# Seven matrix products for eight in more blocks of a hybrid GLA/gMLP layer, with PSUM sums copied from one bank into others

## The chip, the cores and the metric

The kernel runs on one core of one Trainium2 chip. The metric is device time in microseconds (us). Three runs of the kernel before gave 1591.32 us in the median, 1591.16 to 1591.44.

## The reference

One encoder layer on 256 tokens of width 2048, all in fp32. The parts that cost time are products of a 256-row activation with a wide weight matrix:

```python
proj = h @ w_in[i] + b_in[i]                      # 2048 x 14400
q, k, v, og, fg, u, z, ga, gb = jnp.split(proj, pts, axis=-1)
o = gla_chunk_causal(q, k, v, log_a)              # log_a from fg
y_a = rms_norm(o, gla_norm_g[i]).reshape(bsz, s, d) * jax.nn.silu(og)
y_b = gmlp_spatial_gate(gelu(u), gelu(z), gmlp_ln_g[i], gmlp_ln_b[i], w_s[i], b_s[i])
m = jax.nn.sigmoid(ga) * y_a + jax.nn.sigmoid(gb) * y_b
h = layer_norm(ALPHA * h + m @ w_o[i], ln1_g[i], ln1_b[i])      # 2048 x 2048
gt, up = jnp.split(h @ w_gu[i], 2, axis=-1)                     # 2048 x 11264
ffn = (jax.nn.silu(gt) * up) @ w_down[i]                        # 5632 x 2048
ple = jax.nn.sigmoid(h @ w_pg[i] + b_pg[i]) * (p[i] @ w_pu[i])  # 2048 x 2048
h = layer_norm(ALPHA * h + ffn + ple, ln2_g[i], ln2_b[i])
```

## The kernel before, in words

**Products.** Activations are held transposed, in k-tiles of 128 features by 256 tokens, so that a token tile t (0 or 1) of a k-tile is the 128x128 weight of a matmul and 512 columns of a weight matrix stream through. Each fp32 operand is cut into a high part and a low part of the type that TensorE takes (fp32r); a product is three matmuls, high by high, low by high, high by low (`mm3`, lines 275 to 278, and `mul`, 390 to 398).

**Weights.** A weight chunk is two k-tiles by 512 columns (128x1024 in SBUF, 512 KB from HBM, queue SP). Two chunks share one "raw" buffer. `cut` (197 to 204) makes the high part on ScalarE (line 202) and the low part on VectorE (line 203) into a buffer `w`. Raw, cut and long-lived buffers come from one pool of 21 slots.

**Steps.** All work with weights is a list of steps, each with a split (what the cut does) and a use (its matmuls). `pump` (253 to 270) goes through the steps in order. Before the use of step c it emits splits of later steps as long as at most `limit["hl"]` cut buffers are held, and loads as long as at most `limit["raw"]` raw buffers are; after the use it emits one or two jobs. A job is mostly an evacuation: VectorE and ScalarE take a finished PSUM sum, add a bias, apply a function, and so on. `before(c, fn)` puts other work ahead of step c. The queues of SP and GpSimd run as written; ScalarE's up to step 230, which is the end of ga; the rest is put in order by the toolchain, by priority.

**Blocks.** The order is v, fg, q, k, og, z, u, gb, ga, wo, pu, pg (each 2048 columns in four blocks of 512, but for fg, q, k, pu), then four parts of gate/up and down. `token_block` (280 to 333) keeps two PSUM sums, one per token tile, over 8 chunks of 12 matmuls. `pair_block` (366 to 540) takes 512 gate columns and 512 up columns together: four sums C11, C21, C12, C22 (token tile, column block) over 8 pairs of k-tiles. For two of the pairs (`s_gu = 2`, line 1221) it makes seven products in place of eight: it subtracts and adds the four 128x512 weight quarters on VectorE (lines 430, 460, 461), uses sums of the activations that `sums` (335 to 364) made once, and keeps a fifth sum V. What is common to several sums is copied from PSUM to SBUF by ScalarE (lines 451, 452, 512), joined on VectorE (453, 514), and added at each evacuation (1154, 1168). There are 11 such blocks in parts of 3, 3, 3 and 2, with four down blocks (12 or 8 k-tiles) behind each part. PSUM has five banks for these sums (`acc`) and three for the rest (`aux`).

**Around them.** `bcast` (104 to 107) loads 512 elements of a bias or gain to all partitions (three buffers). `residual` (624 to 631) multiplies and adds ln1's gain and bias on GpSimd, called from pg's evacuations (1140). At the start `keep_busy` (643 to 647) fills the wait for x with transposes of the identity.

Of the kernel before, what the change touches and what calls it, by code (L numbers as in the profile page):

```python
# [40 lines left out]
def block_kernel(ctx: ExitStack, tc: tile.TileContext, x, p, ln0_g, ln0_b, w_in, b_in, w_f2, b_f2,  # L41
# [322 lines left out]
    def pair_block(srcs, nk, xT, evacs, name, s, sT):  # L366
# [17 lines left out]
        def bank(key):  # L384
            first = key not in B
            if first:
                B[key] = acc(f"{name}_{key}")
            return B[key], first

        def mul(key, x, w):  # L390
            ps, first = bank(key)
            for j, ((xh, xl), (wh, wl)) in enumerate(zip(x, w)):
                nc.tensor.matmul(ps, lhsT=xh, rhs=wh, start=first and j == 0, stop=False,  # L393
                                 skip_group_check=True)
                nc.tensor.matmul(ps, lhsT=xl, rhs=wh, start=False, stop=False,  # L395
                                 skip_group_check=True)
                nc.tensor.matmul(ps, lhsT=xh, rhs=wl, start=False, stop=True,  # L397
                                 skip_group_check=True)
# [16 lines left out]

        def done(key, t, c):
            left[key] -= 1
            if left[key] == 0:
                add_out(key, B[key], t, c)


        def a1(i, raw):
# [18 lines left out]

        def a2(i, raw, need):
            def split():
                return cut(raw.tile.rearrange("p (q c) -> p q c", c=CB)[:, 0:4:2, :], f"{name}_b{i}")

            def use(w):
                mul("C21", [SX(2, i)], [W(w, 1)])
                mul("C12", [SX(0, i)], [W(w, 0)])
                if i == s - 1:
                    p1, p7 = t2(f"{name}_p1"), t2(f"{name}_p7")  # L450
                    nc.scalar.activation(p1, B["V"], AF.Copy)
                    nc.scalar.activation(p7, B["C21"], AF.Copy)
                    nc.vector.tensor_tensor(out=p7, in0=p7, in1=B["C12"], op=ALU.add)
                    st["p1"], st["h"] = p1, p7
            add_step(split, use, need)

        def tsum(i, raw):
            q = lambda j: raw.tile[:, j * CB:(j + 1) * CB]

            nc.vector.tensor_tensor(out=q(0), in0=q(0), in1=q(3), op=ALU.add)  # L460
            nc.vector.tensor_tensor(out=q(1), in0=q(1), in1=q(0), op=ALU.subtract)


        def std(i, order, sum_of=None):
            raw = Raw()
            n0 = add_half(raw, 0, srcs[0][:, 2 * i:2 * i + 2, :], 2, CB)
            n1 = add_half(raw, 1, srcs[1][:, 2 * i:2 * i + 2, :], 2, CB)
            keys = {(0, 0): "C11", (1, 0): "C21", (0, 1): "C12", (1, 1): "C22"}
            ws = {}

            def mk(c):
                def split():
                    w = cut(raw.tile[:, c * 1024:(c + 1) * 1024], f"{name}_c{i}_{c}")
                    if c == 1 and sum_of is not None:
                        tsum(*sum_of)
                    return w

                def use(w):
                    ws[c] = w
# [800 lines left out]
```

## Time and profile before

| | before |
|---|---|
| runs | 1591.32 us median of 3 (1591.16 to 1591.44) |
| profiled execution | 1591.31 us, its span 1589.5 us |
| mean granted TensorE clock | 0.996 |
| TensorE matmul busy | 1567.8 us, 7442 matmuls |
| VectorE, ScalarE, GpSimd busy | 1062.1, 747.1, 86.5 us |
| HBM read | 312.06 MB, 198 GB/s over the span |

The span is the time between the first and the last instruction that the profiler recorded; 1.8 us of the execution lie outside it. Matmuls overlap in the records (each shows 0.39 us), so the distance of their starts is what one costs, not its duration. VectorE's and ScalarE's instructions overlap by about 0.1 us when one follows another at once.

### The profile page before, as it was taken

Reading aid. Unit: us, or ns where it says so; the run is one execution under the profiler, and the core shown is the slowest. Engines: PE = TensorE matmul, PEld = TensorE weight load, DVE = VectorE, ACT = ScalarE, POOL = GpSimd, SP = SyncE. Lnnn points to the kernel's source line nnn. Section 1 sums busy time; section 2 is a strip of 40 time slices with the busy share of each in tenths; the row PEclk is TensorE's granted clock in tenths of the full one; section 3 lists DMA queues with packets and bytes.
Section 4 is the critical chain, followed back from the end, with each engine's and each line's share of the span. In section 5 each row is a group of like instructions: output and inputs, shape, how many; then the busy total and the mean of one; then the engine's idle time right before and its main releaser. Section 6 shows DMA issues by size and latency. Waiting matters only on the chain.

```text
span 1589.5 us, 19295 instructions
## 1 busy us (share of the span) xinstructions
PE 1567.8 (99%) x7442; PEld 1315.6 (83%) x7442; DVE 1062.1 (67%) x1219; ACT 747.1 (47%) x889; POOL 86.5 (5%) x69
## 2 busy tenths in 40 slices
PE   8999999999999999999999999999999999999996
PEld 7889988888888888888888888888888888888885
DVE  7658456467755556674899776577765777657775
ACT  5435446345543344462744554455544545435440
POOL 1021100001000000000142000000000000000002
PEclk9999999999999999999999999999999999999998
DMA  8664647566656665674577557555565645656551
GB/s 299 200 199 157 215 140 259 192 217 215 200 201 202 222 207 167 223 259 137 187 243 240 180 185 237 179 201 178 184 212 192 227 165 184 211 186 227 172 184 53
DMA packets 164598, 315.43 MB, mean 198 GB/s; under 512 B 10237, under 2 KB 13210, under 8 KB 164250
## 3 DMA queue, kind: packets, MB, share of 16 engines
q1 hardware_dynamic: 164442, 314.19, 58.9%
q8 instruction: 58, 0.95, 0.2%
q14 instruction: 34, 0.28, 0.1%
q10 hardware_dynamic: 64, 0.02, 0.0%
HBM read 312.06 MB, written 2.10 MB: 198 GB/s over the span
## 4 chain that ended last, share of the span: by engine, by line
PE 49%; issue 46%; DVE 3%; POOL 1%; DMA 1%; ACT 0%; SPq 0%; DVEq 0%; POOLq 0%; ACTq 0%
PE og L276 2%; PE v L277 2%; PE og L278 2%; PE v L278 2%; PE ga L278 2%; PE og L277 2%; PE wo L276 2%; PE z L278 2%; PE ga L277 2%; PE u L278 2%; PE wo L277 2%; PE z L277 2%; PE u L277 2%; PE gb L278 2%; PE gb L277 2%
## 5 line engine op out<-in xcount | busy, mean ns | idle before, releaser
L203 DVE TENSOR_TENSOR w_s<-raw,w_s 128x1024 fp32r<-128x1024 f32 x382 | 463.4, 1243 | 167.8 <-ACT w_s L202 167.4
L202 ACT ACTIVATE w_s<-raw 128x1024 fp32r<-128x1024 f32 x382 | 390.5, 1053 | 221.0 <-PE dn L278 72.4
L393 PE MATMUL gu_C<-gu_c_s,h1Th 128*128 128x512 f32 x528 | 205.4, 389 | 0.0
L395 PE MATMUL gu_C<-gu_c_s,h1Tl 128*128 128x512 f32 x528 | 205.4, 389 | 0.0
L397 PE MATMUL gu_C<-gu_c_s,h1Th 128*128 128x512 f32 x528 | 205.4, 389 | 0.0
L203 DVE TENSOR_TENSOR gu_c_s<-raw,gu_c_s 128x1024 fp32r<-128x1024 f32 x132 | 159.2, 1223 | 60.9 <-ACT gu_c_s L202 60.0
L202 ACT ACTIVATE gu_c_s<-raw 128x1024 fp32r<-128x1024 f32 x132 | 137.9, 1059 | 96.5 <-PE gu_C L397 49.3
L276 PE MATMUL dn<-w_s,act 128*128 128x512 f32 (+1 forms) x352 | 136.9, 389 | 0.0
L278 PE MATMUL dn<-w_s,act 128*128 128x512 f32 (+1 forms) x352 | 136.2, 387 | 0.0
L277 PE MATMUL dn<-w_s,act 128*128 128x512 f32 (+1 forms) x352 | 136.1, 387 | 0.0
L397 PEld LDWEIGHTS gu_C<-gu_c_s,h1Th 128*128 128x128 f32 x528 | 99.1, 188 | 20.6
L393 PEld LDWEIGHTS gu_C<-gu_c_s,h1Th 128*128 128x128 f32 x528 | 99.1, 188 | 20.6
L395 PEld LDWEIGHTS gu_C<-gu_c_s,h1Tl 128*128 128x128 f32 x528 | 99.1, 188 | 20.6
L278 PEld LDWEIGHTS dn<-w_s,act 128*128 128x128 f32 x352 | 66.1, 188 | 13.5
L276 PEld LDWEIGHTS dn<-w_s,act 128*128 128x128 f32 x352 | 66.1, 188 | 13.5 <-ACT act L575 0.3
L277 PEld LDWEIGHTS dn<-w_s,act 128*128 128x128 f32 x352 | 66.1, 188 | 13.3
L552 POOL TENSOR_TENSOR ln_r<-ln_v,mhalf 128x1 f32<-128x1 f32 x6 | 4.2, 693 | 1078.5 <-DVE ln_v L547 1078.5
L277 PE MATMUL v<-w_s,h0Tl 128*128 128x512 f32 x128 | 50.0, 391 | 0.9 <-POOL h0Tl L576 0.9
L276 PE MATMUL v<-w_s,h0Th 128*128 128x512 f32 x128 | 50.4, 394 | 0.0
L276 PE MATMUL ga<-w_s,h0Th 128*128 128x512 f32 x128 | 50.4, 394 | 0.0
L276 PE MATMUL og<-w_s,h0Th 128*128 128x512 f32 x128 | 50.2, 392 | 0.0
L276 PE MATMUL wo<-w_s,mTh 128*128 128x512 f32 x128 | 50.1, 391 | 0.0
(296 smaller groups left out, 3152.9 us busy)
## 6 DMA issues: line engine op xcount, KB each, us to landing
raw<-in_w_in_dram SPq DMA_DIRECT2D x226, 512.0 KB, 4.5
raw<-in_w_gu_dram SPq DMA_DIRECT2D x176, 512.0 KB, 4.4
raw<-in_w_down_dram SPq DMA_DIRECT2D x88, 512.0 KB, 4.9
raw<-in_w_o_dram SPq DMA_DIRECT2D x32, 512.0 KB, 5.1
raw<-in_w_pg_dram SPq DMA_DIRECT2D x32, 512.0 KB, 5.0
xs<-in_x_dram SPq DMA_DIRECT2D x4, 512.0 KB, 5.0
raw<-in_w_pu_dram SPq DMA_DIRECT2D x4, 512.0 KB, 4.6
out_dram<-xs SPq DMA_DIRECT2D x8, 256.0 KB, 2.1
```

Source lines behind the costliest of these rows:

```text
L202: nc.scalar.activation(hi, src, AF.Copy)
L203: nc.vector.tensor_tensor(out=lo, in0=src, in1=hi.bitcast(F32), op=ALU.subtract)
L276: nc.tensor.matmul(ps, lhsT=xh, rhs=wh, start=start, stop=False, **kw)
L277: nc.tensor.matmul(ps, lhsT=xl, rhs=wh, start=False, stop=False, **kw)
L278: nc.tensor.matmul(ps, lhsT=xh, rhs=wl, start=False, stop=stop, **kw)
L393: nc.tensor.matmul(ps, lhsT=xh, rhs=wh, start=first and j == 0, stop=False, skip_group_check=True)
L395: nc.tensor.matmul(ps, lhsT=xl, rhs=wh, start=False, stop=False, skip_group_check=True)
L397: nc.tensor.matmul(ps, lhsT=xh, rhs=wl, start=False, stop=True, skip_group_check=True)
L552: nc.gpsimd.tensor_tensor(out=r[:, :n], in0=v[:, :n], in1=mhalf[:, :n], op=ALU.pow)
```

## The change

`pair_block` is rewritten and used in more places. A pair of k-tiles with seven products is now five steps (`sa` to `se`). The product that all four sums share is made once in C12's bank; ScalarE copies C12's bank into the bank of C11 (`seed`), on which TensorE then accumulates, and later, with two further products in it, into the bank of C22; two partial sums go to SBUF (`keep`: `p7` from C21, `v` from C12) and are added at the evacuations of C22 and C21. C11 and C12 have nothing added. The fifth sum V is gone. The other pairs (`std`) are ordinary chunks, and the last chunk of a block is held back (`pending`) until the next block has emitted its `sa` steps (`flush`).

Seven products serve two pairs of k-tiles in og's second two blocks, in u and gb, in ga's first two, in pg's second two blocks, and three pairs in gate/up (before: two). z goes through `pair_block` with none (`S_Z = 0`). Two `sums` are made: of h0's k-tiles for the first, of h1's for pg and gate/up. `rowvec` loads 1024 elements at a time, at a set step ahead of the first use. Evacuations and the copies get a priority 150 instructions earlier. `residual` for ln1 is called at steps 5, 8, 11 and 14 of pg. z's norm takes two instructions in place of three. At the start, 20 fp32 matmuls of the identity go to the five banks in place of 14 transposes. ScalarE runs as written up to two steps before the end of og's first two blocks.

The core of the diff (what `pair_block` loses is printed above; lines that start with a blank stand in both):

```diff
+S_IN, S_Z, S_GA, S_PG, S_FF = 2, 0, 2, 2, 3
+SOON = 150
...
-    def bcast(src, c0, name, n=CB):
+    rows_t = {}
+
+    def rowvec(key, src, c0, b):
+
+        k = key, b // 2
+        if k not in rows_t:
+            rows_t[k] = tmp.tile([P, 2 * CB], F32, tag="bc", name=f"{key}{b // 2}", bufs=3)
+            o = c0 + b // 2 * 2 * CB
+            nc.sync.dma_start(rows_t[k], src[o:o + 2 * CB].partition_broadcast(P))
+        return rows_t[k][:, b % 2 * CB:(b % 2 + 1) * CB]
...
+    pending = []
+    def flush():
+        while pending:
+            pending.pop()()
-        while n > 0 and jobs:
-            jobs.popleft()()
-            n -= 1
+        with tc.high_priority(offset=SOON):
+            while n > 0 and jobs:
+                jobs.popleft()()
+                n -= 1
...
+        def seed(key):
+            B[key] = acc(f"{name}_{key}")
+            with tc.high_priority(offset=SOON):
+                nc.scalar.activation(B[key], B["C12"], AF.Copy)
+        def keep(key, nm):
+            st[nm] = t2(f"{name}_{nm}")
+            with tc.high_priority(offset=SOON):
+                nc.scalar.activation(st[nm], B[key], AF.Copy)
...
+        def done(key):
             left[key] -= 1
             if left[key] == 0:
+                t, c = int(key[1]) - 1, int(key[2]) - 1
+                jobs.append(lambda: evacs[c](t, B[key], st.get({"C21": "v", "C22": "p7"}.get(key))))
+        def q(i, j, n=1):
+            return raws[i].tile[:, j * CB:(j + n) * CB]
+        def sa(i):
+            add_half(raws[i], 0, srcs[0][:, 2 * i:2 * i + 2, :], 2, CB)
+            need_of[i] = add_half(raws[i], 1, srcs[1][:, 2 * i:2 * i + 2, :], 2, CB)
             def split():
+                w = cut(q(i, 0), f"{name}_a{i}", CB)
+                r = raws[i].tile.rearrange("p (q c) -> p q c", c=CB)
+                nc.vector.tensor_tensor(out=r[:, 0:4:2, :], in0=r[:, 0:4:3, :],
+                                        in1=r[:, 2, :].unsqueeze(1).broadcast_to([P, 2, CB]),
                                         op=ALU.subtract)
                 return w
             def use(w):
+                mul("C12", [X(i, 0, 0)], [W(w)])
+                if i == s - 1:
+                    seed("C11")
+            add_step(split, use, need_of[i])
+        def sb(i):
+            def p2(j):
+                mul("C11", [X(j, 1, 0)], [W(wb[j], 0)])
+                done("C11")
+            def use(w):
+                wb[i] = w
+                mul("C21", [SX(2, i)], [W(w, 1)])
+                if i:
+                    p2(i - 1)
+                if i == s - 1:
+                    keep("C21", "p7")
+                    p2(i)
+            n = add_step(lambda: cut(q(i, 1, 2), f"{name}_b{i}"), use, need_of[i], (),
+                         None if i == s - 1 else True)
+            if i:
+                steps[n]["free_hl"] += 1
+        def sc(i):
             def split():
+                nc.vector.tensor_tensor(out=q(i, 2), in0=q(i, 0), in1=q(i, 3), op=ALU.add)
+                w = cut(q(i, 2), f"{name}_c{i}", CB)
+                nc.vector.tensor_tensor(out=q(i, 1), in0=q(i, 1), in1=q(i, 2), op=ALU.subtract)
+                return w
             def use(w):
+                mul("C12", [SX(1, i)], [W(w)])
+                if i == s - 1:
+                    keep("C12", "v")
+            add_step(split, use, need_of[i])
+        def sd(i):
+            def use(w):
                 mul("C12", [SX(0, i)], [W(w, 0)])
                 if i == s - 1:
+                    seed("C22")
                 mul("C21", [X(i, 1, 1)], [W(w, 1)])
+                done("C21")
+            add_step(lambda: cut(q(i, 0, 2), f"{name}_d{i}"), use, need_of[i])
+        def se(i):
+            def use(w):
+                mul("C12", [SX(3, i)], [W(w)])
+                done("C12")
+            add_step(lambda: cut(q(i, 3), f"{name}_e{i}", CB), use, need_of[i], (raws[i],))
+        def std(i, c):
+            def consume(hi, lo):
+                w = [(hi[:, o * CB:(o + 1) * CB], lo[:, o * CB:(o + 1) * CB]) for o in range(2)]
+                for t in range(NT):
+                    mul(f"C{t + 1}{c + 1}", [X(i, 0, t), X(i, 1, t)], w)
+                    done(f"C{t + 1}{c + 1}")
+            add_chunk(srcs[c][:, 2 * i:2 * i + 2, :], 2, CB, consume)
+        c0 = [(lambda i=i: std(i, 0)) for i in range(s, npair)]
+        c1 = [(lambda i=i: std(i, 1)) for i in range(s, npair)]
         if s:
+            todo = [lambda i=i: sa(i) for i in range(s)] + [flush]
+            todo += [lambda i=i: sb(i) for i in range(s)]
+            todo.append(c0.pop(0))
+            todo += [lambda i=i: sc(i) for i in range(s)]
+            todo.append(c0.pop(0))
+            todo += [lambda i=i: sd(i) for i in range(s)]
+            for i in range(s):
+                if c0:
+                    todo.append(c0.pop(0))
+                todo.append(lambda i=i: se(i))
+                if len(c1) > 2 or not c0:
+                    todo.append(c1.pop(0))
+            todo += c0 + c1
+        else:
+            todo = [flush] + [f for x in zip(c0, c1) for f in x]
+        for f in todo[:-1]:
+            f()
+        pending.append(todo[-1])
...
+    def soon(n, fn):
+        before(len(steps) + n, fn)
+    def pairs(w, c0, xT, evac, name, s, sT, bs=(0, 2), vecs=()):
+        for b in bs:
+            for key, src, o in vecs:
+                soon(8, lambda key=key, src=src, o=o, b=b: rowvec(key, src, o, b))
+            pair_block((wcols(w, c0 + b * CB), wcols(w, c0 + (b + 1) * CB)), KT, xT,
+                       (evac(b), evac(b + 1)), f"{name}{b}", s, sT)
...
-        keep_busy(14, "busy0")
+        banks = [acc(f"init{i}") for i in range(5)]
+        for j in range(4):
+            for i in range(5):
+                nc.tensor.matmul(banks[i][:, j * P:(j + 1) * P], lhsT=ident, rhs=ident,
+                                 start=j == 0, stop=j == 3, skip_group_check=True)
...
+        nc.vector.tensor_tensor(out=a, in0=ps, in1=rowvec(f"b_{key}", src, c0, b), op=ALU.add)
+    soon(4, lambda: rowvec("b_og", b_in, C_OG, 0))
+    for b in range(2):
+    n_act = len(steps) - 2
+    before(len(steps) - 3, lambda: G.update(s0=sums(h0T, S_IN, "s0")))
+    before(len(steps), lambda: limit.update(raw=4, hl=5))
+    pairs(w_in, C_OG, h0T, og_evac, "og", S_IN, s0, (2,), [("b_og", b_in, C_OG)])
+                                           in1=rowvec("gmg", gm_g, 0, b), op0=ALU.subtract,
+                                           in1=rowvec("gmb", gm_b, 0, b), op0=ALU.mult, op1=ALU.add)
...
+            later(7, parts)
+            later(11, mix)
+    pairs(w_in, C_Z, h0T, z_evac, "z", S_Z, s0, (0, 2), [("b_z", b_in, C_Z), ("gmg", gm_g, 0), ("gmb", gm_b, 0)])
+    pairs(w_in, C_U, h0T, lambda b: yb_evac("u", C_U, b, AF.Gelu), "u", S_IN, s0, (0, 2), [("b_u", b_in, C_U)])
+    pairs(w_in, C_GB, h0T, lambda b: yb_evac("gb", C_GB, b, AF.Sigmoid), "gb", S_IN, s0, (0, 2), [("b_gb", b_in, C_GB)])
...
-    for b in range(4):
+    before(len(steps), lambda: limit.update(raw=3, hl=4))
+    pairs(w_in, C_GA, h0T, ga_evac, "ga", S_GA, s0, (0,), [("b_ga", b_in, C_GA)])
+    soon(2, lambda: rowvec("b_ga", b_in, C_GA, 2))
+    for b in range(2, 4):
...
-    for b in range(4):
+    for c in range(4):
+        soon(5 + 3 * c, lambda c=c: residual(ln1_g, ln1_b, c, "ln1"))
+    soon(3, lambda: rowvec("b_pg", b_pg, 0, 0))
+    for b in range(2):
-    s_gu = 2
-    before(len(steps) - 16, lambda: G.update(s1=sums(h1T["x"], s_gu, "s1")))
-    before(len(steps), lambda: limit.update(raw=5, hl=5))
+    before(len(steps) - 4, lambda: G.update(s1=sums(h1T["x"], S_FF, "s1")))
+    before(len(steps), lambda: limit.update(raw=S_FF + 2, hl=5))
+    pairs(w_pg, 0, h1T_get, pg_evac, "pg", S_PG, s1, (2,), [("b_pg", b_pg, 0)])
-            if s_gu:
-                pair_block((wcols(w_gu, j * CB), wcols(w_gu, DFF + j * CB)), KT, h1T_get,
-                           (gate_evac(j), up_evac(j, part, i * 4)), f"gu{j}", s_gu,
-                           lambda: G["s1"])
-            else:
-                token_block(wcols(w_gu, j * CB), KT, h1T_get, gate_evac(j), f"gt{j}")
-                token_block(wcols(w_gu, DFF + j * CB), KT, h1T_get, up_evac(j, part, i * 4), f"up{j}")
+            pair_block((wcols(w_gu, j * CB), wcols(w_gu, DFF + j * CB)), KT, h1T_get,
+                       (gate_evac(j), up_evac(j, part, i * 4)), f"gu{j}", S_FF, s1)
-        pump(230)
+        pump(n_act)
```

## Rows read from the trace of the kernel before

**Rows 1.** The page, part 1: busy us (share of span) and instructions of each engine.
```profile
PE 1567.8 (99%) x7442; PEld 1315.6 (83%) x7442; DVE 1062.1 (67%) x1219; ACT 747.1 (47%) x889; POOL 86.5 (5%) x69
```
**Rows 2.** Timeline of PE: start us, us, instruction; within ga, then the starts of two gate/up blocks.
```profile
600.14 0.39 PE L276 MATMUL ga<-w_s,h0Th 128*128 128x512 f32 x1
...
602.86 0.39 PE L276 MATMUL ga<-w_s,h0Th 128*128 128x512 f32 x1
...
859.70 0.39 PE L393 MATMUL gu_C<-gu_a_s,h1Th 128*128 128x512 f32 x1
...
901.86 0.39 PE L393 MATMUL gu_C<-gu_a_s,h1Th 128*128 128x512 f32 x1
```
**Rows 3.** Windows (z, pg, gate/up): PE, PEld, DVE, ACT, POOL; clock, DMA, GB/s.
```profile
313.00:405.00 92.00, 92.00 (x406) 75.96 (x405) 63.86 (x85) 44.90 (x55) 8.39 (x6) 1.00 0.63 206
777.00:860.00 83.00, 83.00 (x369) 68.72 (x368) 78.03 (x76) 39.74 (x47) 33.49 (x16) 1.00 0.68 228
903.00:946.00 43.00, 43.00 (x195) 35.63 (x194) 33.58 (x36) 23.25 (x27) 0.00 (x0) 1.00 0.57 194
831.00:837.00 6.00, 6.00 (x28) 4.99 (x27) 6.00 (x4) 2.17 (x3) 5.84 (x4) 1.00 0.71 237
849.00:855.00 6.00, 6.00 (x28) 4.95 (x28) 5.97 (x4) 1.55 (x2) 4.24 (x3) 1.00 0.83 289
866.00:872.00 6.00, 6.00 (x28) 4.95 (x28) 5.91 (x7) 3.07 (x4) 0.00 (x0) 1.00 0.99 348
```
**Rows 4.** Timelines of DVE and ACT in a gate/up block: two instructions back to back.
```profile
906.86 2.36 DVE L203 TENSOR_TENSOR gu_c_s<-raw,gu_c_s 128x1024 fp32r<-128x1024 f32 x2 [0.26 <-ACT gu_c_s L202]
936.90 1.29 DVE L460 TENSOR_TENSOR raw<-raw 128x512 f32<-128x512 f32 x2
905.76 2.01 ACT L202 ACTIVATE gu_c_s<-raw 128x1024 fp32r<-128x1024 f32 x2
```
**Rows 5.** Lines by form, whole span: busy us, mean ns | idle before, releaser.
```profile
L452 ACT ACTIVATE gu_p<-gu_C 128x512 f32<-128x512 f32 x11 | 6.6, 597 | 0.0
L202 ACT ACTIVATE gu_c_s<-raw 128x1024 fp32r<-128x1024 f32 x132 | 137.9, 1059 | 96.5 <-PE gu_C L397 49.3 <-DVE gu_c_s L203 19.9 <-DVE gu_e_s L203 19.7
L203 DVE TENSOR_TENSOR gu_c_s<-raw,gu_c_s 128x1024 fp32r<-128x1024 f32 x132 | 159.2, 1223 | 60.9 <-ACT gu_c_s L202 60.0
L203 DVE TENSOR_TENSOR gu_e_s<-raw,gu_e_s 128x512 fp32r<-128x512 f32 x22 | 15.1, 684 | 0.0
```
**Rows 6.** Timeline of pg, DVE and POOL: a cut beside GpSimd, the activation sums.
```profile
793.87 1.22 DVE L203 TENSOR_TENSOR w_s<-raw,w_s 128x1024 fp32r<-128x1024 f32 x1
798.43 2.31 DVE L203 TENSOR_TENSOR w_s<-raw,w_s 128x1024 fp32r<-128x1024 f32 x1
805.27 1.21 DVE L344 TENSOR_TENSOR s_full<-h1Th,h1Tl 128x1024 f32<-128x1024 f32 x1
806.93 0.42 DVE L355 TENSOR_TENSOR s_f<-s_full 128x256 f32<-128x256 f32 x1
811.40 1.23 DVE L363 TENSOR_TENSOR s_s<-s_f,s_s 128x1024 fp32r<-128x1024 f32 x1 [1.19 <-ACT s_s L362]
798.03 1.63 POOL L631 TENSOR_TENSOR xs<-xs,ln1b 128x512 f32<-128x512 f32 x1
```
**Rows 7.** Timeline of the start, PE and DVE, and of fp32 matmuls of 256 columns.
```profile
1.36 3.25 PE L647 MATMUL busy<-ident 128*128 128x128 f32 x14 [1.36 <-POOL ident masks.py:199]
8.56 0.45 PE L640 MATMUL rows_ps<-ident,rows_rows 128*128 128x128 f32 x1 [3.95 <-POOL ln_r L552]
8.80 2.77 PE L647 MATMUL busy<-ident 128*128 128x128 f32 x12
11.43 1.08 PE L569 MATMUL h0t_ps<-ident,xs 128*128 128x128 f32 x4
12.90 1.37 DVE L582 TENSOR_SCALAR h0t<-h0t_ps,rows_cols 128x128 f32<-128x128 f32 x4
119.54 1.13 PE L787 MATMUL f_ps<-fgT,wf 64*128 64x256 f32 x4
```

More of the change, by code (lines that the diff above doesn't have):

```diff
@@ L376, in pair_block, with mul @@
         npair = nk // 2
-        st = {}
-        sq = [(i, Raw()) for i in range(s)]
-        B, left = {}, {"C11": npair, "C21": npair, "C12": npair, "C22": npair - s}
+        st, B, wb = {}, {}, {}
+        left = {"C11": npair, "C21": npair, "C12": npair, "C22": npair - s}
+        raws = [Raw() for i in range(s)]
+        need_of = {}
         def x_of():
             return xT() if callable(xT) else xT
-        def bank(key):
+        def mul(key, x, w):
             first = key not in B
@@ L387, in bank @@
                 B[key] = acc(f"{name}_{key}")
-            return B[key], first
-        def mul(key, x, w):
-            ps, first = bank(key)
+            ps = B[key]
             for j, ((xh, xl), (wh, wl)) in enumerate(zip(x, w)):
[L393 to L398, printed above, removed]
+                for n, (a, b) in enumerate(((xh, wh), (xl, wh), (xh, wl))):
+                    nc.tensor.matmul(ps, lhsT=a, rhs=b, start=first and j == 0 and n == 0,
+                                     stop=n == 2, skip_group_check=True)
+        def seed(key):
[6 more added lines that the diff above has]
+                nc.scalar.activation(st[nm], B[key], AF.Copy)
         def X(i, o, t):
@@ L448, in use @@
+        def sd(i):
+            def use(w):
                 mul("C12", [SX(0, i)], [W(w, 0)])
                 if i == s - 1:
[L450 to L461, printed above, removed]
@@ L464, in std @@
[L464 to L479, printed above, removed]
-                    todo = order.get(c, ())
-                    for t, cc in todo:
-                        k = keys[t, cc]
-                        mul(k, [X(i, 0, t), X(i, 1, t)], [W(ws[cc], 0), W(ws[cc], 1)])
-                        done(k, t, cc)
-                return split, use
-            sp, us = mk(0)
-            late = any(cc == 0 for _, cc in order.get(1, ()))
-            add_step(sp, us, n0, (), True if late else None)
-            sp, us = mk(1)
-            n = add_step(sp, us, n1, (raw,))
-            if late:
-                steps[n]["free_hl"] += 1
@@ L519, in x_cols @@
-        def x_cols(c):
-            return c
-        need_of = {}
-        if s:
-            need_of[0] = a1(*sq[0])
-            for i in range(1, s):
-                need_of[i] = a1(*sq[i])
-                a2(*sq[i - 1], need_of[i - 1])
-            a2(*sq[s - 1], need_of[s - 1])
-        normal = {0: ((0, 0), (1, 0)), 1: ((0, 1), (1, 1))}
-        first = {0: ((0, 0),), 1: ((1, 1), (1, 0), (0, 1))} if s else normal
-        rest = list(range(s, npair))
-        sum_at = {j: sq[j] for j in range(s)}
@@ L533, in pair_block @@
-        nb = 0
-        for j, i in enumerate(rest):
-            std(i, first if j == 0 else normal, sum_at.get(j))
-            if s and j >= 1 and nb < s and nb <= j - 1 and j < len(rest) - 1:
-                b(*sq[nb])
-                nb += 1
-        assert nb == s
+                    seed("C22")
+                mul("C21", [X(i, 1, 1)], [W(w, 1)])
+                done("C21")
[5 more added lines that the diff above has]
+            add_step(lambda: cut(q(i, 3), f"{name}_e{i}", CB), use, need_of[i], (raws[i],))
@@ L1130, in block_kernel, with s1 @@
     r1 = h0
-    res_done = set()
+    def s1():
+        return G["s1"]
     def pg_evac(b):
@@ L1137, in evac @@
             cs = slice(b * CB, (b + 1) * CB)
-            if b not in res_done:
-                res_done.add(b)
-                residual(ln1_g, ln1_b, b, "ln1")
-            a = biased(t, ps, f"pg{b}", b_pg, b * CB, add)
+            a = biased(t, ps, "pg", b_pg, 0, b, add)
             nc.scalar.activation(a, a, AF.Sigmoid)
```

93 lines of the change are left out of this document (16 added, 77 removed).

## The prediction

> **What bounds the kernel now.** I read the page's table of engines first, then the timeline of TensorE, then windows by stage, then the mean of each kind of instruction. The table shows matmuls busy for 99% of the span and VectorE for 67% [rows 1]. Busy matmuls overlap, so that alone proves no bound; the timeline does. In ga twelve matmuls start within 602.86 - 600.14 = 2.72 us, 0.2267 us each, and a whole gate/up block takes 901.86 - 859.70 = 42.16 us [rows 2]. Such a block has 8 pairs x 8 products x 3 matmuls less 2 x 3 = 186 matmuls, and 186 x 0.2267 = 42.16: not one gap in it, although VectorE does seven-product work in it. The windows say the same of z, pg and gate/up: the clock column reads 1.00, so TensorE is at its 2.4 GHz level throughout, and over each whole stage every other engine has idle time [rows 3]. So TensorE's issue sets the end, and a matmul less is worth 0.2267 us, as long as the cuts arrive.
>
> **What the change removes.** One product of three matmuls for each converted pair of k-tiles. Gate/up: 11 blocks x 1 more pair x 3 = 33. og one pair of blocks x 2 x 3 = 6, u 12, gb 12, ga 6, pg 6; z none. Together 75, and 75 x 0.2267 = 17.0 us [rows 2].
>
> **What it adds to VectorE and ScalarE.** Back to back, a 1024-element VectorE instruction costs 2.36 - 1.22 = 1.14 us, a 512-element one 1.29 - 0.68 = 0.61, called 0.60, a ScalarE cut of 1024 2.01 - 1.06 = 0.95 [rows 4, 5]. A converted pair needs `sa` 0.60 + 1.14, `sb` 1.14, `sc` 3 x 0.60, `sd` 1.14, `se` 0.60: 6.4 us of VectorE beside 21 x 0.2267 = 4.76 us of matmuls. An ordinary pair needs 2.28 beside 5.44. A gate/up block becomes 3 x 6.4 + 5 x 2.28 + six evacuation instructions of 0.60 = 34.2 us of VectorE against 183 x 0.2267 + 0.9 for its transposes = 42.4 of TensorE: 81%, where the windows show 33.6 of 43.0 now [rows 3]. A block of u: 2 x 6.4 + 6 x 2.28 + 6.0 = 32.5 against 42.2. So on average VectorE fits, and ScalarE, at some 25 us a block, with room.
>
> Locally it is tight, at the opening of a block. From the first `sa` until the second ordinary chunk is wanted, TensorE of gate/up has 2.04 (three `sa`), 2.72 (the held-back chunk), 4.08 (`sb`), 2.72, 2.04 (`sc`) and 0.9 of transposes: 14.5 us. VectorE owes for the same stretch 5.2 + 1.14 + 3.4 + 1.14 + 5.4 + 1.14 and five evacuation instructions, 3.0: 20.5 us. With five cut buffers it can have the three `sa` and the held-back chunk, 6.4 us, done before TensorE enters: the steps ahead of the opening give it 2.72 + 0.68 + 2.72 + 2.72 = 8.8 us for these and one evacuation, 7.0. Left are 14.1 of 14.5 us; with `sb` ahead too, 13.0. So the margin is 0.4 to 1.5 us, and I take no loss; the bound is 1 us in each of the 7 openings that follow another gate/up block, 7 us. In u and gb the same count is 10.9 against 15.8 - 6.9 = 8.9, margin 2.0. In z all four sums end together, about 4 x 3.3 us of VectorE, in a stage with 28 of 92 us free [rows 3]: nothing.
>
> `seed` is a ScalarE copy from PSUM to PSUM, of which there is no row; the nearest are the copy from PSUM to SBUF, 0.60, and a cut, 1.06 [rows 5]. I take 0.60. The first seed has the held-back chunk and `sb`'s first product, 3.4 us, before TensorE writes that bank; behind a cut in progress it needs 1.06 + 0.60 + 0.17 (the tail of the matmul that it waits for) = 1.83. The second has 0.68 + 2.72. `keep` of p7 is the closest: C21 is written again after nine matmuls, 2.04 us, against 1.83. If a copy came 0.4 us late in each of the 18 converted blocks this would cost 7 us; the waiting matmul would hold all that follows it on TensorE. Taken: 0.
>
> **The pg stage.** Here VectorE has only 83.0 - 78.0 = 5.0 us free, since its cuts stretch beside GpSimd's `residual`: 2.31 us against 1.22 [rows 3, 6]. The change adds two converted pairs to it, 2 x (6.4 - 2.28) = 8.2 us, and a third pair in the sums of the activations. For two pairs these took from 805.27 to 812.6 us, 7.3 us partly beside GpSimd [rows 6]; for three 1.5 x 7.3 = 11.0. They are now emitted four chunks before the converted block and are first used two `sa` steps into it: 4 x 2.72 + 2 x 0.68 = 12.2 us. VectorE also owes cuts in that time, but may start earlier, being up to three chunks ahead. `residual` moves to steps 5 to 14, so half of GpSimd's 33 us falls into the ordinary blocks; there the load of the second ln1 pair waits on SP for GpSimd to free two of three buffers, with three raw buffers, six chunks or 16 us, already issued. Bounds 0 and 8 us; I take 1.0, nearer to nothing, because VectorE was full late in this stage too (6.00 and 5.97 us of two windows of 6) while TensorE issued its usual 28 matmuls in each [rows 3]. The first sums, for og, take 1.21 + 4 x 0.42 + 1.06 + 1.23 = 5.2 us and have 3 x 2.72 + 1.36 = 9.5 [rows 5, 6]: nothing.
>
> The Trainium skill ("SBUF — State Buffer", Who interferes with whom) says that VectorE with two SBUF inputs and a GpSimd instruction that reads SBUF lock each other out for a whole instruction. The 2.31 us cut, 0.4 us behind the start of a GpSimd addition, agrees. By that rule alone half of the 16 GpSimd instructions could each hold one instruction of the converted block, and the sum would stand at the upper bound, near 1582.6; by the two full windows it stays at the lower one.
>
> **The rest.** The toolchain orders ScalarE from og on; gate/up runs like that now without a gap: nothing, but up to 1 us a stage if a late activation function holds cuts. Weight bytes are unchanged; the heaviest call is 3.7 MB from the cut of the second `se` to that of the last `sa`, about 12.9 us or 284 GB/s, and 348 GB/s are seen [rows 3]. At the start, an fp32 matmul that is no transpose is two instructions (the row of line 787 shows four for its last two calls), so 20 make 40 where 14 were; at the 0.22 us of the first transposes they end at 1.36 + 40 x 0.22 = 10.2 us, and the rows' transpose slips from 8.56 [rows 7]. The twelve fillers behind it then end at 13.0 and h0's transposes, now 11.43, at 13.9, 1.0 us past the 12.90 at which VectorE takes them up. At the 0.113 us per 128 columns that line 787 shows later, they end near 6 and nothing slips. Bounds 0 to 1.0; I take 0.3.
>
> **The sum**, against the profiled execution's 1591.31 us (span 1589.5 and 1.8 outside it), which is the median of the runs to 0.01: 1591.3 - 17.0 + 1.0 + 0.3 = 1575.6 us.
>
> **The rivals.** First, GpSimd and the converted block collide in pg. The stage then lacks 8.2 + 3.7 (sums) + 1.4 (less matmul time) - 5.0 = 8.3 us, or the openings lose 0.5 to 1 us each: 1574.3 + 8.3 = 1582.6, range 1579 to 1585. For it speaks VectorE's 94% there; against, that the two full windows cost nothing. The page named above says the same in general terms.
>
> Second, the other side: VectorE becomes the bound at the openings. If only two of the cuts are ahead, because buffers come free late (of the 21 slots 2 hold the residual stream, 4 h1's k-tiles, now 2 the sums and up to 3 the gate/up results, which leaves 10), 20.5 - 3.5 = 17.0 us stand against 14.5: 2.5 us in each of 11 blocks, 27.5 us, so 1602. It decides from 17.0 / 11 = 1.55 us per block. For it speaks that a converted pair costs VectorE 6.4 us for TensorE's 4.76; against, that the block in the rows holds two such pairs without a gap [rows 2].
>
> Third, the change doesn't do what it says: the saved products come back as waits for `seed` and `keep`, 0.9 us in each of 18 blocks, 17 us: no change.
>
> **How the numbers follow.** Forecast 0.65 (its own range 1574 to 1579: no loss at all, up to 3 us more than taken), pg or slight losses 0.19, openings 0.12 (of it faster 0.02, within 0.2% 0.03, slower 0.07), no gain 0.04. A measurement of this kernel tells 0.2%, 3.2 us, from no change. Faster 0.65 + 0.19 + 0.02 = 0.86, same 0.03 + 0.04, slower 0.07. The range takes in the forecast, half a microsecond below its end for a sum that is a little off, and the first rival, and leaves out the others, 0.16: 1573.5 to 1585.
>
> **What would show it.** 75 fewer 512-column matmuls, still 0.2267 us apart; gate/up block starts 41.5 + 0.9 us apart; no idle of TensorE in front of `sc` or the chunk behind it; in pg no wait of a matmul for the sums; VectorE near 80% in gate/up. The prediction is wrong if TensorE waits for cuts (line 203's successor) at each opening, if `seed` or `keep` heads the list of what TensorE waits for, or if VectorE takes up h0's first transposes later than 12.90 us.

## The result and the profile after

| | before | after |
|---|---|---|
| runs | 1591.36 us median | 1605.81 us median of 4 (1602.99 to 1607.29) |
| ratio | | 1.0089, 95% interval 1.0071 to 1.0106 |
| profiled execution, its span | 1591.31, 1589.5 us | 1605.97, 1603.8 us |

The change made the kernel slower by 14.4 us, where 15.7 us less were predicted. The page's table of engines (busy us, share, instructions) answers to [rows 1]:

```profile
PE 1565.2 (98%) x7393; PEld 1306.4 (81%) x7393; DVE 1159.4 (72%) x1359; ACT 817.5 (51%) x1026; POOL 92.5 (6%) x69
```

The count is right: 7442 - 75 + 26 (the 40 records at the start for 14) = 7393. So the time went into gaps. I measured each stage in TensorE's timeline, from its first matmul to the next stage's first. "By the sum" is before less 0.2267 us for each matmul saved, and corrected for what only changes its stage: a converted block's held-back chunk (2.72 us) runs behind the first matmuls of a converted block that follows. The last row runs from gate/up's first matmul to the end of the last matmul. "Pg undone" is `e8_pg_tokens`, below; nothing of pg is saved or held back there, so its loss is counted against 88.91 in pg and 706.85 in the last row.

| stage | before | by the sum | after | lost | pg undone, lost |
|---|---|---|---|---|---|
| q | 50.30 | 50.30 | 56.29 | 6.0 | 0.0 |
| og | 103.31 | 101.95 | 102.50 | 0.5 | 0.5 |
| z and u | 179.89 | 174.45 | 179.51 | 5.1 | 0.8 |
| gb | 87.04 | 84.32 | 84.32 | 0.0 | 0.0 |
| pg | 88.91 | 84.83 | 100.69 | 15.9 | 0.0 |
| gate/up and down | 714.33 | 709.57 | 712.67 | 3.1 | 1.3 |

With 0.8 us in ga, wo, pu and the start these losses are 31.4 us; less 17.0 saved, 14.4.

The list of what TensorE waited for (engine, line, releaser; us in total, times, longest) names three of the places; before, it held nothing behind the start of v:

```profile
PE pg_C L408 <- ACT pg_C L414: 4.4, 1, 4.4
PE q L292 <- DVE w_s L218: 4.0, 2, 2.6
PE pg_C L408 <- DVE pg_b_s L218: 2.5, 1, 2.5
PE u_C L408 <- DVE w_s L218: 2.4, 1, 2.4
PE pg L293 <- DVE w_s L218: 2.3, 1, 2.3
...
PE pg_C L408 <- ACT pg_b_s L217: 1.2, 1, 1.2
...
PE u_C L408 <- DVE u_c_s L218: 0.5, 1, 0.5
PE gu_C L408 <- ACT gu_c_s L217: 0.3, 1, 0.3
```

The waits alone are 4.0 us in q, 2.9 in u and 10.4 in pg; the stages lost 6.0, 5.1 and 15.9. The windows (columns as in [rows 3]: z, pg, gate/up, then stretches of q, pg and u, and q behind its waits) show the rest:

```profile
318.00:405.00 87.00, 87.00 (x385) 71.97 (x384) 53.75 (x67) 38.39 (x44) 4.61 (x4) 1.00 0.59 202
775.00:875.00 100.00, 89.55 (x380) 72.29 (x379) 87.98 (x92) 48.26 (x62) 39.51 (x16) 0.93 0.53 181
892.00:935.00 43.00, 42.95 (x192) 34.77 (x191) 34.81 (x41) 25.91 (x35) 0.00 (x0) 1.00 0.55 194
148.00:154.00 6.00, 3.42 (x27) 3.22 (x28) 5.44 (x18) 0.41 (x1) 0.00 (x0) 1.00 0.00 0
829.00:841.00 12.00, 6.00 (x14) 4.16 (x15) 12.00 (x16) 6.59 (x11) 0.47 (x1) 0.58 0.09 23
419.00:425.00 6.00, 4.20 (x11) 3.32 (x12) 6.00 (x8) 3.21 (x4) 0.00 (x0) 0.72 0.51 169
155.00:158.40 3.40, 3.40 (x19) 3.40 (x18) 3.40 (x4) 3.15 (x4) 0.00 (x0) 0.50 0.11 14
```

Behind these waits the granted clock fell to its 1.2 GHz level (0.50 in the last window; 0.58 and 0.72 are means of stretches at both levels), and there the distance of 512-column matmuls is 0.43 us, not 0.2267. In q the clock was still full between 148 and 154, where the second wait lies, and fell behind it. Gate/up holds: 34.8 us of VectorE in 43, and its blocks start 42.45 us apart, against [rows 2]:

```profile
1112.45 0.39 PE L408 MATMUL gu_C<-gu_a_s,h1Th 128*128 128x512 f32 x1
...
1154.90 0.39 PE L408 MATMUL gu_C<-gu_a_s,h1Th 128*128 128x512 f32 x1
```

In pg, the timelines of VectorE, ScalarE and GpSimd answer to [rows 6]: the activation sums from their first to their last instruction, cuts, the subtractions of `sa`, the queue to the first `seed` (line 414).

```profile
807.51 2.84 DVE L360 TENSOR_TENSOR s_full<-h1Th,h1Tl 128x1536 f32<-128x1536 f32 x1
...
816.04 2.29 DVE L379 TENSOR_TENSOR s_sl<-s_f,s_sh 128x1536 fp32r<-128x1536 f32 x1 [1.62 <-ACT s_sh L378]
818.25 2.28 DVE L218 TENSOR_TENSOR w_s<-raw,w_s 128x1024 fp32r<-128x1024 f32 x1
820.46 3.44 DVE L218 TENSOR_TENSOR pg_a_s<-raw,pg_a_s 128x512 fp32r<-128x512 f32 x2
823.82 4.53 DVE L448 TENSOR_TENSOR raw<-raw 128x1024 f32<-128x1024 f32 x2
...
834.02 0.68 DVE L985 TENSOR_TENSOR a_pg<-pg,b_pg 128x512 f32<-128x512 f32 x1
834.73 0.63 ACT L1148 ACTIVATE a_pg<-a_pg 128x512 f32<-128x512 f32 x1 [4.30 <-DVE a_pg L985]
835.26 1.13 ACT L217 ACTIVATE pg_c_s<-raw 128x512 fp32r<-128x512 f32 x2
836.30 0.58 ACT L414 ACTIVATE pg_C<-pg_C 128x512 f32<-128x512 f32 x1
...
827.34 2.13 POOL L635 TENSOR_TENSOR xs<-xs,ln1b 128x512 f32<-128x512 f32 x1
```

Until GpSimd ends, at 829.5, VectorE takes 2.28 us for 1.2, 3.44 for 1.3, 4.53 for 2.35. The seed is done in 0.58 us, but stands behind an evacuation's function, which waits 4.3 us for VectorE, and behind two cuts. No cut and no matmul of the stage waits for a weight load; of the engines that compute GpSimd alone waits for a DMA.

### The profile page after: what moved, and what is told of

It reads as the page before. It is cut to its first block, busy times and chain, and to the rows that moved or that the text cites. A ratio compares the mean times of both kernels' runs of the same rounds, so it can differ in the third digit from the quotient of the medians.

```text
span 1603.8 us, 19476 instructions
## 1 busy us (share of the span) xinstructions
PE 1565.2 (98%) x7393; PEld 1306.4 (81%) x7393; DVE 1159.4 (72%) x1359; ACT 817.5 (51%) x1026; POOL 92.5 (6%) x69
## 4 chain that ended last, share of the span: by engine, by line
issue 48%; PE 22%; POOL 2%; DVE 2%; DMA 1%; ACT 0%; SPq 0%; POOLq 0%
PE gb_C L408 5%; PE u_C L408 5%; PE ga_C L408 3%; PE wo L293 2%; PE wo L291 2%; PE wo L292 2%; PE ga L292 1%; PE ga L291 1%; PE ga L293 1%; POOL xs L635 1%; POOL xs L634 1%; DVE xs L1206 0%; DMA ln1g<-in_ln_g_dram 0%; DVE xs L1204 0%; PE mtp L574 0%
## 5 line engine op out<-in xcount | busy, mean ns | idle before, releaser
L218 DVE TENSOR_TENSOR w_s<-raw,w_s 128x1024 fp32r<-128x1024 f32 x464 | 564.4, 1231 | 283.6 <-ACT w_s L217 280.6
L217 ACT ACTIVATE w_s<-raw 128x1024 fp32r<-128x1024 f32 x464 | 482.8, 1056 | 396.2 <-PE dn L293 94.4
L408 PE MATMUL gu_C<-w_s,h1Th 128*128 128x512 f32 x880 | 283.7, 390 | 0.2
L408 PEld LDWEIGHTS gu_C<-w_s,h1Th 128*128 128x128 f32 x880 | 165.0, 188 | 35.2 <-DVE w_s L218 1.4
L408 PE MATMUL gu_C<-w_s,h1Tl 128*128 128x512 f32 x440 | 171.6, 390 | 0.0
L408 PEld LDWEIGHTS gu_C<-w_s,h1Tl 128*128 128x128 f32 x440 | 82.6, 188 | 17.1
L408 PE MATMUL z_C<-w_s,h0Th 128*128 128x512 f32 x256 | 79.6, 389 | 0.0
L408 PE MATMUL u_C<-w_s,h0Th 128*128 128x512 f32 x192 | 62.4, 396 | 2.4 <-DVE w_s L218 2.4
L408 PE MATMUL gb_C<-w_s,h0Th 128*128 128x512 f32 x192 | 61.1, 389 | 0.0
L448 DVE TENSOR_TENSOR raw<-raw 128x1024 f32<-128x1024 f32 x47 | 58.5, 1266 | 0.5
L291 PE MATMUL v<-w_s,h0Th 128*128 128x512 f32 x128 | 50.4, 394 | 0.0
```

The costliest lines, as they stand in the source:

```text
L217: nc.scalar.activation(hi, src, AF.Copy)
L218: nc.vector.tensor_tensor(out=lo, in0=src, in1=hi.bitcast(F32), op=ALU.subtract)
L291: nc.tensor.matmul(ps, lhsT=xh, rhs=wh, start=start, stop=False, **kw)
L408: nc.tensor.matmul(ps, lhsT=a, rhs=b, start=first and j == 0 and n == 0, stop=n == 2, skip_group_check=True)
L448: nc.vector.tensor_tensor(out=r[:, 0:4:2, :], in0=r[:, 0:4:3, :], in1=r[:, 2, :].unsqueeze(1).broadcast_to([P, 2, CB]), op=ALU.subtract)
```

## The experiments

**One cause taken away in each.**

`e1_ln0_late`:
```diff
-        before(30 + 5 * c, lambda c=c: residual(ln0_g, ln0_b, c, "ln0"))
+        before((30, 35, 60, 65)[c], lambda c=c: residual(ln0_g, ln0_b, c, "ln0"))
```


> The third and fourth 512-column groups of GpSimd's ln0 gain and bias are taken up at steps 60 and 65 and not at 40 and 45, after the decay scans. Theory (GpSimd beside the scans makes VectorE slow, cuts come late, TensorE waits and its clock falls): the 19 first scans take about 3.5 us and not 8.9, the q stage goes from 56.3 back to about 50.3 us, the whole to about 1600. Rival (the q stage is longer for something else, the wider gain and bias loads or the order of ScalarE's work): the q stage stays at 56 us and the whole at 1605 to 1606.

1600.22 us, q 50.30: the theory. VectorE's timeline in the changed kernel, 19 of the 32 scans of 64 columns, with GpSimd busy until 144.35, and the cut behind them:

```profile
137.77 8.92 DVE L816 TENSOR_TENSOR_SCAN dmn<-dmn,dlg 128x64 f32<-128x64 f32 x19
146.61 1.19 DVE L218 TENSOR_TENSOR w_s<-raw,w_s 128x1024 fp32r<-128x1024 f32 x1
```

The last 17 scans here, with GpSimd idle:

```profile
137.70 3.20 DVE L816 TENSOR_TENSOR_SCAN dmn<-dmn,dlg 128x64 f32<-128x64 f32 x17
```

VectorE's order changed too: the cut behind 19 scans stands behind ten here, as before the change. No run separates the two; at 0.19 us each, nineteen scans would take 3.6 us.

`e2_ln1_late`:
```diff
-        soon(5 + 3 * c, lambda c=c: residual(ln1_g, ln1_b, c, "ln1"))
+        soon((5, 8, 27, 30)[c], lambda c=c: residual(ln1_g, ln1_b, c, "ln1"))
```


> The third and fourth groups of GpSimd's ln1 gain and bias come at 27 and 30 steps after the pg stage's start and not at 11 and 14, so behind the opening of the converted pg block. Theory (GpSimd, one stretch of 42 us, doubles VectorE's work at that opening): the pg stage goes from 100.7 to 88 to 91 us and the whole to 1593 to 1596; VectorE's two-input instructions at the opening halve. Rival (the four sums of chunks, made only four steps ahead, and ScalarE's order behind them make the wait by themselves): the stage stays at 97 us or more, the whole at 1602 or more.

1602.2 us: neither. pg fell to 93.7 us, but gate/up to its end rose by 4.1, since the last two groups now ran in its first block's opening. In pg the first two groups, done at 810.94, still slowed the sums. The opening behind them ran at its own pace, as the theory had it, but late, and a seed waited 4.7 us: 8.8 of the 15.9 us stayed lost.

```profile
817.32 1.29 DVE L218 TENSOR_TENSOR pg_a_s<-raw,pg_a_s 128x512 fp32r<-128x512 f32 x2
818.52 2.35 DVE L448 TENSOR_TENSOR raw<-raw 128x1024 f32<-128x1024 f32 x2
...
PE pg_C L408 <- ACT pg_C L414: 4.7, 1, 4.7
```

`e3_z_tokens`:
```diff
-    pairs(w_in, C_Z, h0T, z_evac, "z", S_Z, s0, (0, 2), [("b_z", b_in, C_Z), ("gmg", gm_g, 0), ("gmb", gm_b, 0)])
+    for b in range(4):
+        token_block(wcols(w_in, C_Z + b * CB), KT, h0T, z_evac(b), f"z{b}")
...
-            later(7, parts)
-            later(11, mix)
+            later(3, parts)
+            later(5, mix)
```


> z is computed as four single blocks again, with its later work 3 and 5 steps behind, so that its evacuations come two by two. Theory (z's four evacuations together fill VectorE and ScalarE at u's opening): the waits of 2.4 and 0.5 us at the start of u and the low clock behind them go, the whole falls by about 5 us to about 1601. Rival (u's opening is short of time by its own cuts and subtractions): the wait at u's start stays at 2 us or more and the whole within 1.5 us of 1605.8.

1601.44 us: the theory, 4.4 us. z and u together take 175.27 us and both waits in u are gone.

`e4_pg_plain`:
```diff
-S_IN, S_Z, S_GA, S_PG, S_FF = 2, 0, 2, 2, 3
+S_IN, S_Z, S_GA, S_PG, S_FF = 2, 0, 2, 0, 3
```


> The second pair of pg's blocks is computed with all products (6 matmuls more, 1.4 us), still as a pair. Theory of the collision (the converted block's opening beside GpSimd): the 15.9 us that the pg stage lacks fall to 0 to 5, the stage to 90 to 93 us and the whole to 1594 to 1598. Rival (GpSimd's stretch, SyncE's blocked loads and the late sums hold back any block here): the stage stays at 98 us or more and the whole at 1603 or more.

1598.13 us, pg 91.9: just past the theory's upper end. Plain products in the same place save 8.8 us of the stage; about 5.7 stay lost, with waits of 2.3 and 1.3 us.

**Which part of pg.**

`e5_sums_early`:
```diff
-    before(len(steps) - 4, lambda: G.update(s1=sums(h1T["x"], S_FF, "s1")))
+    before(len(steps) - 12, lambda: G.update(s1=sums(h1T["x"], S_FF, "s1")))
```


> Only the sums of chunks for pg and gate/up are made eight steps earlier (twelve steps ahead of the converted pg block and not four). Theory (in pg two things meet: GpSimd's stretch and the late sums, whose chain over VectorE and ScalarE holds the next cuts back): the wait for the cut ahead of the converted block goes, the pg stage falls from 100.7 to 93 to 96 us and the whole to 1598 to 1601. Rival (GpSimd alone; the sums only fill time that VectorE has): the stage stays at 98 us or more and the whole at 1603 or more.

1607.18 us, pg 101.9: my theory fell. The wait of 2.3 us ahead of the converted block is gone, but its opening, beside GpSimd, is as late as ever (7.0 us of waits), and TensorE waits 4.1 us at the start of pg, where ScalarE's cut is late behind the sums, with GpSimd still idle.

`e6_no_ln1` leaves ln1's gain and bias out of the result:
```diff
-    for c in range(4):
-        soon(5 + 3 * c, lambda c=c: residual(ln1_g, ln1_b, c, "ln1"))
```


> ln1's gain and bias on GpSimd are left out altogether (16 GpSimd instructions and their four loads), the rest is as in the changed kernel. Rival (GpSimd is the whole cause in pg): VectorE's two-input instructions at the opening run at their own pace, the pg stage falls to 85 to 88 us and the whole to 1590 to 1593. Theory (sums and GpSimd share it): the stage stays at 89 to 94 us, with a wait for the first seed or a cut of 1 us or more, and the whole at 1595 to 1599.

1590.82 us, pg 84.84, the 84.83 of the sum: the rival, without GpSimd's work nothing is lost in pg. The windows of pg and of its converted opening have no gap and full clock; sums at the same steps hurt nobody. Their last instruction, shown below the windows, ends 34.2 us into the stage, and 43.3 in the changed kernel:

```profile
774.00:858.00 84.00, 84.00 (x380) 69.53 (x379) 73.65 (x92) 47.85 (x61) 0.00 (x0) 1.00 0.57 190
818.00:842.00 24.00, 24.00 (x108) 19.88 (x107) 18.20 (x21) 16.30 (x21) 0.00 (x0) 1.00 0.72 245
...
805.71 1.76 DVE L379 TENSOR_TENSOR s_sl<-s_f,s_sh 128x1536 fp32r<-128x1536 f32 x1 [1.62 <-ACT s_sh L378]
```

`e7_all_moved`, the edits of `e1_ln0_late`, `e3_z_tokens` and `e5_sums_early`, and:
```diff
-        soon(5 + 3 * c, lambda c=c: residual(ln1_g, ln1_b, c, "ln1"))
+        soon((5, 8, 22, 25)[c], lambda c=c: residual(ln1_g, ln1_b, c, "ln1"))
```


> All three together, and nothing of the seven products taken back: ln0's groups after the scans, z in single blocks, pg's sums eight steps earlier and the last two ln1 groups behind the opening of the converted pg block. Theory (the three causes add up): 1605.8 less 5.6, less 4.4 and less 10 to 15 for pg: 1581 to 1586, faster than before. Rival (pg's converted block lacks time by itself): 1590 or more.

1587.47 us, 0.9975 (0.9966 to 0.9985): faster than before, 1.5 us short of the theory. The opening is free of waits; the early sums cost their 4.1 us again (pg 91.9):

```profile
PE pg L291 <- ACT w_s L217: 4.1, 1, 4.1
```

`e8_pg_tokens`, with the edits of `e1_ln0_late` and `e3_z_tokens`:
```diff
-    for c in range(4):
-        soon(5 + 3 * c, lambda c=c: residual(ln1_g, ln1_b, c, "ln1"))
...
+            if b not in res_done:
+                res_done.add(b)
+                residual(ln1_g, ln1_b, b, "ln1")
...
-    pairs(w_pg, 0, h1T_get, pg_evac, "pg", S_PG, s1, (2,), [("b_pg", b_pg, 0)])
+    for b in range(2, 4):
+        token_block(wcols(w_pg, b * CB), KT, h1T_get, pg_evac(b), f"pg{b}")
+    before(len(steps) - 16, lambda: G.update(s1=sums(h1T["x"], S_FF, "s1")))
```


> As the kernel with ln0's groups after the scans and z in single blocks, but with pg as it was before: four single blocks with all products, ln1's gain and bias in the evacuations, and the sums sixteen steps ahead of gate/up. Theory: the pg stage is back at 88 to 90 us; against before 69 matmuls fewer (15.6 us), about 3.4 us lost in small gaps of gate/up and 1 us in u: 1579 to 1582. Rival (the saved products are lost wherever blocks are converted): 1588 or more.

1579.18 us, ratio 0.9926 (0.9909 to 0.9942): the theory, and the fastest version, ahead of both kernels. GpSimd works 30.9 us in pg here too, beside ordinary blocks, and TensorE has no gap (window of pg):

```profile
765.00:853.00 88.00, 88.00 (x398) 72.84 (x397) 79.72 (x82) 43.32 (x53) 30.88 (x16) 1.00 0.61 213
```

**The mechanism, and the price of gate/up's third pair.**

`e9_ln1_dve`; `e10_all_dve` takes 5, 8, 27 and 30 for 5 + 3 * c and the edits of `e1_ln0_late` and `e3_z_tokens`:
```diff
-        soon(5 + 3 * c, lambda c=c: residual(ln1_g, ln1_b, c, "ln1"))
+        soon(5 + 3 * c, lambda c=c: residual(ln1_g, ln1_b, c, "ln1", nc.vector))
```


> ln1's gain and bias are taken over by VectorE, at the same steps (16 instructions of 128x512 more on VectorE, by its 0.6 to 0.7 us some 10 us, and none on GpSimd). Theory (what hurts in pg is that VectorE's two-input instructions double beside GpSimd, which is dearer than the work itself): VectorE's cuts of 1,024 columns take 1.2 us again, the pg stage falls from 100.7 to 85 to 90 us, the whole to 1591 to 1596. Rival (VectorE has too little time at that opening, whoever does the work): the stage stays at 95 us or more, the whole at 1600 or more.

> The version that the theory points to: ln0's groups after the scans, z in single blocks, ln1 on VectorE with its last two groups behind the converted pg block's opening; all of pg's and the other products saved, sums where they were. Theory: pg stage 85 to 87 us; of the 17.0 us saved about 3.4 lost in gate/up and 1 in u: 1577 to 1580, below the kernel with pg undone (1579.2) or equal to it. Rival (the work on VectorE comes back as late cuts in pg or at the first gate/up block): 1583 or more.

The first: 1594.91 us, pg 91.6: the time is the theory's, the stage 1.6 us above it (in the profiled execution, the longest of the six with 1598.48). The same work on VectorE costs pg 9 us less than on GpSimd beside it, and 6.8 us more than none. The second: 1587.36 us, the rival: its last two groups meet gate/up's first opening, where TensorE waits for cuts (1.4, 1.3, 0.8, 0.7 and 0.4 us). VectorE has room for that work at neither opening.

`e11_gu_two` is `e8_pg_tokens` with `S_FF = 2`.

> As the kernel with ln0 late, z and pg in single blocks, but two pairs of k-tiles converted in gate/up and not three. By my sum the third pair is worth 33 matmuls of 0.2267 us, 7.5 us. Theory (it is worth that less the small gaps at the openings, 2 to 3 us): 1579.2 plus 4 to 6: 1583 to 1585. Rival (VectorE is the bound at the openings with three pairs and eats the saving): 1577 to 1580.

1586.32 us, 7.1 more; from gate/up's first matmul to the end 715.70 us against 708.12, 7.6. Both beyond the theory: the third pair is worth its 7.5 us almost or quite in full, and the small gaps are there with two pairs as well (1.4 us, for 1.3 with three).

`e12_ln_singles`:
```diff
-        gt, bt = rowvec(f"{name}g", g, 0, c), rowvec(f"{name}b", b, 0, c)
+        def one(src, key):
+            t = tmp.tile([P, 2 * CB], F32, tag="bc", name=f"{name}{key}{c}", bufs=3)[:, :CB]
+            nc.sync.dma_start(t, src[c * CB:(c + 1) * CB].partition_broadcast(P))
+            return t
+        gt, bt = one(g, "g"), one(b, "b")
```


> Only the gain and bias rows of ln0 and ln1 are loaded 512 columns at a time, as before the change, and not 1,024; all steps stay. Theory (one wide load for two groups lets GpSimd go through two groups without a pause, in the scans of q and in pg): the fourth ln0 group waits for its own load as before, q goes back to 50 to 51 us and pg to 90 to 97: the whole at 1590 to 1599. Rival (the new steps alone put the work there, the loads set nothing): q stays at 54 to 56 us, pg at 99 to 102, the whole at 1603 to 1607.

1599.85 us: q is the theory's, 50.4, pg the rival's, 100.7. In GpSimd's timeline the fourth ln0 group waits for its load again, as before the change (second row); in the changed kernel it followed at 138.97 without a wait (third row):

```profile
161.25 1.29 POOL L638 TENSOR_TENSOR xs<-xs,ln0g 128x512 f32<-128x512 f32 x1 [23.61 <-DMA ln0g<-in_ln_g_dram]
...
159.62 1.71 POOL L630 TENSOR_TENSOR xs<-xs,ln0g 128x512 f32<-128x512 f32 x1 [22.02 <-DMA ln0g<-in_ln_g_dram]
...
138.97 1.28 POOL L634 TENSOR_TENSOR xs<-xs,ln0g 128x512 f32<-128x512 f32 x1
```

**Can pg keep its seven products?**

`e13_evac_pairs` has only the first two parts of the diff of `e8_pg_tokens`; `e14_spread` has the edits of `e1_ln0_late` and `e3_z_tokens`, 4, 10, 22 and 25 for 5 + 3 * c, and the sums nine steps ahead for four.

> The changed kernel with ln1's four GpSimd groups called in pg's evacuations, as before the change; the converted block, the joined loads and the late sums stay. Theory (the early steps 5, 8, 11 and 14 put GpSimd's stretch on the converted block's opening): only the first two groups touch the opening, the pg stage falls from 100.7 to 88 to 93 us and the whole to 1594 to 1599. Rival (the converted block can't stand beside GpSimd's work wherever that lies): the stage stays at 95 us or more and the whole at 1600 or more.

> All products of the change kept: ln0's groups after the scans, z in single blocks, ln1's groups at 4, 10, 22 and 25 steps into pg, the sums seven steps into pg (five later than in the run that met a wait at the stage's start, five earlier than in the changed kernel). Theory: no wait over 1 us in pg, its stage 85 to 88 us, gate/up to the end as in the run without ln1's work: 1579 to 1582, the same as with pg undone (1579.2), since the first gate/up block gives back what pg's six products save. Rival (the sums beside GpSimd hold the cuts back again): pg 90 us or more, the whole 1584 or more.

The first: 1606.05 us. pg falls to 92.95, but gate/up pays 9.6 us: by the wide loads, the last two groups come at once and late, 859.58 to 874.3, on its opening. The second: 1584.54 us, pg 89.2 with no wait in its converted block. But at the stage's start, where GpSimd's first two groups (761.4 to 777.2) now meet the cuts of h1 and of pg's first weights, TensorE waits 2.2 us for a cut and 0.8 and 0.5 us for h1; the theory, no wait over 1 us, is missed. The time is the rival's, its mechanism is not: the sums come when GpSimd is idle.

```profile
PE pg L293 <- DVE w_s L218: 2.2, 1, 2.2
...
786.55 1.75 DVE L360 TENSOR_TENSOR s_full<-h1Th,h1Tl 128x1536 f32<-128x1536 f32 x1
```

It stays 5.4 us above pg undone. Narrow loads together with the evacuations, and the converted block, was not tried.

## Why the prediction was wrong

**The failed step is the pg stage**, taken at 1.0 us between 0 and 8; it lost 15.9. The collision was named as the first rival, and without GpSimd's work the loss is 0.0 (`e6_no_ln1`). Three things made it dearer than my bound. I counted VectorE's work over the whole stage, but the converted block needs it in order and ahead of time: first the sums and the cuts, then its opening. GpSimd, busy up to 829.5, slowed both. With its last two groups away from the opening, 8.8 and 8.1 us stayed lost, for VectorE came late to it (`e2_ln1_late`, `e13_evac_pairs`); the other 7 us came with the last two groups beside the opening. The queues passed the delay on: the seed behind a function that waited for VectorE. And the clock fell behind the waits, 10.4 us of them for 15.9 lost. I had chosen the lower end by two windows in which VectorE was full while TensorE missed nothing; those were ordinary blocks, whose cuts have slack, as `e8_pg_tokens` shows. The Trainium skill's rule ("SBUF — State Buffer", Who interferes with whom), that VectorE with two SBUF inputs and a GpSimd instruction that reads SBUF lock each other out for a whole instruction, agrees with the traces: such a cut took 2.28 us beside GpSimd (818.25) and 1.21 without it (834.62), and in the kernel before an addition with one input in PSUM took 0.68 us beside GpSimd (796.72), one with both in SBUF 1.78 (795.01).

**A step was missing: q**, 6.0 us. I had looked at the wide loads for SP's wait in pg only. In ln0 the narrow load had held the fourth group back until after the scans; the joined one let GpSimd run from 132.75 to 144.35 beside them (`e1_ln0_late`, `e12_ln_singles`). Of the 6.0 us 4.5 are VectorE's delay: in five later runs with the same q the clock stayed full behind the same waits, and the stage took 54.8 us.

**z, taken as nothing**, cost 4.2 of u's 5.1 us. I had compared its four evacuations with the free time of z's stage; they run in u's opening, whose margin of 2.0 us I had worked out with 3.0 us of evacuations, not 13.

**What held.** A matmul is worth 0.2267 us, and 33 fewer in gate/up 7.1 to 7.6, for 7.5 by the sum (`e11_gu_two`). The openings, the second rival: gate/up blocks are 42.45 us apart for 42.4 predicted. The time came near that rival's 1602 by chance, not by its mechanism. `seed` and `keep` take 0.58 and 0.59 us for 0.60, and are hidden wherever VectorE is in time, but for 0.3 us in gate/up with pg undone, so that the third rival did not come; a seed does head the list of waits, one of my signs of being wrong, but by one block of 18. The start cost 0.04 us for 0.3: the 40 records took 6.37 us, 0.16 each; h0's first transposes ran at 11.37 and VectorE took them up at 12.93, for 12.90 before. The small gaps of gate/up I had not priced: 3.1 us, 1.8 of them gone with pg undone. What makes the other 1.3, the 0.5 in og and the 0.8 in ga, wo and pu stays open.

With q and z mended and pg undone, 69 matmuls fewer (15.6 us) and 3.5 us of small losses (2.6 in the table's last column, the rest in ga, wo and pu) give 1591.3 - 15.6 + 3.5 = 1579.2, the measured 1579.18.

## What to carry to other kernels

Price new work at the place where it needs its input ahead of time, not against the stage's mean; a full VectorE is harmless in a block with slack, but sets the end in an opening, and work beside ordinary blocks is not free either if it leaves VectorE late for an opening behind them. When a load is widened or moved, ask what it had been holding back: a late DMA can be the only thing that keeps two engines apart. The price of a short wait of TensorE is not fixed: 4.0 us of waits cost q 4.5 us in five runs and 6.0 in three, by the clock behind them, and 10.4 us cost pg 15.9. And pg's six matmuls, 1.4 us, are not worth a collision: even with GpSimd's work left out, pg and what follows take 797.5 us, against 797.0 with pg undone, for gate/up then lacks 1.8 us more.

## What was not expected of the hardware

- Scans of 64 columns took 0.47 us each beside GpSimd (8.92 for 19) and 0.19 without it (3.20 for 17). The 0.47 is a mean of two kinds: of the seven that started before GpSimd ended, five took 1.31 to 1.38 us, about one GpSimd instruction (1.28 to 1.35), and two 0.26 like the rest. In proportion short instructions suffer more than wide ones.
- After the same wait the clock fell in some runs and not in others. After 0.87 us at the start of v, the matmuls went on 0.2267 us apart in some and at first 0.42 to 0.60 apart in others: v took 91.3 us in `e8_pg_tokens` and 92.9 in `e9_ln1_dve`. After q's waits of 1.4 and 2.6 us the changed kernel's clock was 0.50 (window 155.00:158.40 above), and that of `e5_sums_early` 1.00, where q took 54.8 us for 56.3:

```profile
154.50:158.00 3.50, 3.50 (x32) 3.50 (x31) 3.50 (x4) 3.50 (x4) 0.00 (x0) 1.00 0.08 12
```
